# The end of a convolution mixer by token halves, with an activation that names the next function's table and an order edge on one product

## The chip, the cores and the metric

The kernel runs on one core of one Trainium2 chip. The metric is the device time of one execution in microseconds (us). The core has five engines with a queue each: TensorE (PE) multiplies matrices, VectorE (DVE), ScalarE (ACT) and GpSimd (POOL) work on vectors, and SyncE (SP) issues the transfers. Each takes its instructions in the order in which they stand in its queue, and waits on semaphores for what other engines hand it.

## The reference, cut to what matters

The network is a long chain of layers; the change touches the conformer mixer of its second block (and, by an order edge that moves nothing, one product of the first block's indexer). For 256 tokens and 1024 channels the mixer is

```python
a, g = jnp.split(h @ w_in + b_in, 2, axis=-1)
u = a * jax.nn.sigmoid(g)
u = lax.conv_general_dilated(u, w_dw[:, None, :], window_strides=(1,),
        padding=[(CONV_WIDTH - 1, 0)], feature_group_count=D_MODEL, ...) + b_dw
mu = jnp.mean(u32, axis=-1, keepdims=True)
var = jnp.mean(jnp.square(u32 - mu), axis=-1, keepdims=True)
u = (u32 - mu) * lax.rsqrt(var + LN_EPS) * ln_g + ln_b
return jax.nn.silu(u) @ w_out + b_out
```

So there is a product with 2048 outputs, a gate, a causal depthwise convolution of 31 taps per channel, a layer norm over the channels of each token, a Silu, and a second product.

## The kernel before, in words

The 1024 channels are eight blocks of 128, one channel per partition. All products are made in three passes, from a high and a low part of each operand (helper mm3, lines 203 to 205: high by high, high by low, low by high). Weights arrive through SyncE in pieces of 1 MB (tile raw, two buffers); ScalarE casts each half of a piece to its high part (L149) and VectorE subtracts that to get the low part (L152). For the last weights of the mixer (w2, w3) GpSimd does the subtraction.

The first product runs block by block. For each block TensorE sums a and g, ScalarE makes the sigmoid (tile sg, L1428) and VectorE the gated u (tiles ud, up, L1429). Blocks 0 to 3 are made in an earlier loop, in token halves, blocks 4 to 7 one after the other; the weights of block 7 have the tiles ws_12396 and ws_12399 in the listings below.

The 31 taps of the convolution are divided among the engines:

- VectorE has two lanes that it takes in turn, blocks 1 and 3, then blocks 2 and 4 and one tap of block 5: one instruction per tap over all 256 tokens (L1393, the first tap of a block L1395, the tap of block 5 L1397, tile part).
- GpSimd has block 0 and 14 taps of block 5 (tile pw).
- TensorE has blocks 6 and 7 and the last 16 taps of block 5, as products with diagonal matrices. ScalarE makes each diagonal matrix from the identity (tile diag, eight buffers, L1367 and L1377). Blocks 6 and 7 come out with channels on partitions (L1368: one product of 256 columns in two passes) and go to the tile cv by ScalarE (L1370). The 16 taps of block 5 come out with tokens on partitions: one product per token half, t0 and t1 (L1379).

At the end each block is turned to token rows by TensorE (stats, L1462 for one summand, L1465 for several); VectorE takes the statistics (bst, L1479 and L1481), ScalarE copies the rows out (tile rows, L1478 and L1482). norm_c makes mean and factor on VectorE and GpSimd and normalizes the rows on VectorE (L1552). silu_c turns them back on TensorE (L1558), ScalarE applies the Silu (L1562), and the second product follows (mm3 on ws of wcout).

What stands in which order is set by two things. A string PLAN lists the steps of the end: w is a weight to load, d some taps of VectorE, p and q the diagonal products of a block, t and r the row products of block 5, s the turning of a block. The framework then schedules each instruction by its own rules into the queue of its engine, as far as data, buffers and order edges allow: after(i, j) makes i follow j, and in_turn chains the products of the end on TensorE. Nothing else ties a diagonal matrix, a subtraction or a tap to its place in the text.

Of the kernel before, what the change touches and what calls it, by code (L numbers as in the profile page):

```python
# [9 lines left out]
F32 = mybir.dt.float32  # L10
# [4 lines left out]
AF = mybir.ActivationFunctionType  # L15
# [4 lines left out]
D = 1024  # L20
# [8 lines left out]
P_CW, P_CB, P_BA, P_BX, P_LAM, P_BIN, P_DB, P_LG, P_LB, P_DW = 0, 4, 5, 6, 7, 8, 10, 11, 12, 13  # L29
# [10 lines left out]


NTAP = (16, 16, 16, 16)
PLAN = "w0 w1 d64 p6: w2 d32 p7:20 s1 s2 s0 s6 q7:20 d999 t5:2 s7 r5:2 w3 s3 s4 s5"
ROWS = tuple(int(w[1]) for w in PLAN.split() if w[0] == "s")
LAG = 3
KACT = 1
GATE = 1
# [2 lines left out]
KS = 1  # L50
KQ = 14
WPOOL = 2
# [16 lines left out]
def _body(nc, tc, ctx, a, out, dbg):  # L69
# [17 lines left out]
    def ps(tag):  # L87
        return pp.tile([128, 512], F32, name=tag, tag=tag, bufs={"pm": 2, "pt": 2, "pa": 4}[tag])
# [69 lines left out]
    st = Stream()  # L158

    def after(i, j):  # L160
        tc.add_manual_dep(i.ins, j.ins.name, mybir.DependencyInfo(mybir.DependencyClass.NoSync, mybir.DependencyReason.DATA), reason="order")
# [36 lines left out]
    def cut(pair, c):  # L198
        return tuple(v.rearrange("p (c w) -> p c w", c=c) for v in pair)

    def mm3(o, wp, xp, first, last):
        (wh, wl), (xh, xl) = wp, xp
        nc.tensor.matmul(o, wh, xh, start=first, stop=False)  # L203
        nc.tensor.matmul(o, wh, xl, start=False, stop=False)  # L204
        nc.tensor.matmul(o, wl, xh, start=False, stop=last)  # L205

    def split_to(hi, lo, src):
        split_to.last = nc.scalar.activation(hi, src, AF.Copy)  # L208
# [112 lines left out]
    def rows_src(w, n):  # L321
        v = w.rearrange("(n c p) d -> n p c d", c=2, p=128)
        return [v[i] for i in range(n)]
# [5 lines left out]
    with ExitStack() as s1:  # L329
# [12 lines left out]
        def tmp(name, shape, bufs=2, dt=F32):  # L342
            return bp.tile(shape, dt, name=name, tag=name, bufs=bufs)
# [14 lines left out]
        ident = load_const("ident", [128, 128], a["ident"])  # L358
# [18 lines left out]
        pv = load_const("pv", [128, NPV, 8], a["pv"])  # L377
# [16 lines left out]
        r = rstd([xm[:NM]], D, bp, NM)  # L394
# [85 lines left out]
        az, sden, s2, acc_, mx, l8 = (ls[:, i, :] for i in range(6))  # L480
# [171 lines left out]
        scale = 96.0 ** -0.5  # L652
# [130 lines left out]
    with ExitStack() as s2:  # L783
# [259 lines left out]
        def first_queries():  # L1043

            p = [ps("pa") for _ in range(2)]
            pairs = [cut(pair, 4) for pair in st.units(a["wpq"][0])]
            for t in range(2):
                for ob in range(2):
                    o = p[ob][:, 256 * t:256 * t + 256]
                    s = slice(ob * 128, ob * 128 + 128)  # L1050
                    for c in range(8):
                        wh, wl = (v[:, c % 4, s] for v in pairs[c // 4])
                        v = xT[0].tiles[c // 4][:, c % 4, :, 128 * t:128 * t + 128]
                        if c == 7:
                            nc.tensor.matmul(o[:, 0:128], wl, v[:, 0], start=False, stop=False)
                        nc.tensor.matmul(o.rearrange("p (k t) -> p k t", k=2), wh, v, start=c == 0, stop=c == 7)
                        if c < 7:
                            nc.tensor.matmul(o[:, 0:128], wl, v[:, 0], start=False, stop=False)
                    dst = qT[:, ob, 128 * t:128 * t + 128]
                    nc.scalar.activation(dst, o[:, 128:256], AF.Copy)  # L1060
                    nc.vector.tensor_tensor(out=dst, in0=o[:, 0:128], in1=dst, op=ALU.add)
# [11 lines left out]
        for n in range(64):  # L1073
            cn = C[:, 2 * n:2 * n + 2, :]
            hb = cp.tile([128, 2, T], F32, name="hb", tag="hb", bufs=2)
            for u, pair in enumerate(st.units(a["peer_u"][n])):
                p = ps("pa")
                wh, wl = cut(pair, 8)
# [64 lines left out]
    with ExitStack() as s3:  # L1143
# [195 lines left out]
        cv = Q([128, 8, T], F32, "cv")  # L1339
# [13 lines left out]
        turn = {}  # L1353
# [6 lines left out]
        def dwconv_pe(b, k0, k1):  # L1360
            u = uslot(b)
            if k0 == 0:
                parts[b] = [cv[:, b, :]], ps("pm")
            p = parts[b][1]
            for k in range(k0, k1):
                dg = tmp("diag", [128, 128], 8)
                turn["act"] = nc.scalar.activation(dg, ident, AF.Copy, scale=pv[:, P_DW + k, b:b + 1])  # L1367
                in_turn(nc.tensor.matmul(p[:, :T], dg, u[:, k:k + T], start=k == 0, stop=k == 30))  # L1368
            if k1 == 31:
                nc.scalar.activation(cv[:, b, :], p[:, :T], AF.Identity, bias=pv[:, P_DB, b:b + 1])  # L1370
                parts[b] = parts[b][0]

        def dwconv_rows(b, k0, k1):
            u = uslot(b)
            for k in range(k0, k1):
                dg = tmp("diag", [128, 128], 8)
                turn["act"] = nc.scalar.activation(dg, ident, AF.Copy, scale=pv[:, P_DW + k, b:b + 1])  # L1377
                for t in range(2):
                    in_turn(nc.tensor.matmul(rows_at(b, t), u[:, k + t * 128:k + t * 128 + 128], dg, start=k == KQ + KS, stop=False))  # L1379

        def taps(lane):
# [49 lines left out]
        dsteps = together(VL)  # L1431
# [6 lines left out]
        order = []  # L1438
# [12 lines left out]
                return p[:, (i - 4) * 256 + t * 128:(i - 4) * 256 + t * 128 + 128]  # L1451
            return p[:, t * 128:t * 128 + 128]

        def stats(b):

            n = len(order)
            assert ROWS[n] == b
            order.append(b)
            for t in range(2):
                src = [v[:, t * 128:(t + 1) * 128] for v in parts[b]]  # L1460
                if len(src) == 1:
                    in_turn(nc.tensor.transpose(rows_at(b, t), src[0], ident))  # L1462
                    continue
                for i, v in enumerate(src):
                    in_turn(nc.tensor.matmul(rows_at(b, t), v, ident, start=i == 0 and b != 5, stop=i == len(src) - 1))  # L1465
            if n not in ENDS:
                return
            i = n
            f, n = ENDS[i]
            c = i // 2 - 1 if i < 6 else i - 4  # L1470
            for t in range(2):
                dst = rows[:, t, f * 128:(f + n) * 128]
                src = rows_at(b, t)
                if i == 3:
                    src = banks[0][t]
                elif i == 5:
                    src = banks[4][t].rearrange("p (b t c) -> p b t c", b=2, t=2)[:, :, t, :]
                    nc.scalar.activation(dst.rearrange("p (b c) -> p b c", b=2), src, AF.Copy)  # L1478
                    nc.vector.bn_stats(bst[:, t, c, :], dst)  # L1479
                    continue  # L1480
                nc.vector.bn_stats(bst[:, t, c, :], src)  # L1481
                nc.scalar.activation(dst, src, AF.Copy)  # L1482
# [29 lines left out]
        def run_steps(g, n=999):  # L1512
            for _ in range(n):
                if next(g, 0) == 0:
                    return
# [6 lines left out]
                taps_pool(5, 6, KQ)  # L1522
        wco = []

        srcs = rows_src(a["wcout"], 4)
        for w in PLAN.split():
            if w[0] == "w":
                st.gate = turn.get("act")
                wco.append(st.units(srcs[int(w[1:])], eng=nc.gpsimd, behind=turn["pool"]) if int(w[1:]) >= WPOOL else st.units(srcs[int(w[1:])]))
                st.gate = None  # L1530
            elif w[0] == "p":
                dwconv_pe(int(w[1]), 0, int(w[3:] or 31))
            elif w[0] == "q":
                dwconv_pe(int(w[1]), int(w[3:]), 31)
            elif w[0] == "r":
                dwconv_rows(int(w[1]), KQ + KS + int(w[3:] or 0), 31)
            elif w[0] == "t":
                dwconv_rows(int(w[1]), KQ + KS, KQ + KS + int(w[3:]))
            elif w[0] == "d":
                run_steps(dsteps, int(w[1:]))  # L1540
            else:
                stats(int(w[1:]))
        dump("cv", cv)
        def norm_c(t):
            mv = small.tile([128, 2], F32, name="mv", tag="mv", bufs=2)
            nc.vector.bn_aggr(mv, bst[:, t, :, :])
            rs = small.tile([128, 1], F32, name="rsc", tag="rsc", bufs=2)
            nc.vector.tensor_scalar(rs, mv[:, 1:2], 1e-5, None, ALU.add)
            nc.gpsimd.tensor_tensor(out=rs, in0=rs, in1=mhalf, op=ALU.pow)
            for half in range(2):  # L1550
                s = slice(half * 512, half * 512 + 512)
                nc.vector.tensor_scalar(rows[:, t, s], rows[:, t, s], mv[:, 0:1], rs, ALU.subtract, ALU.mult)  # L1552
# [10 lines left out]
                c = slice(4 * half, 4 * half + 4)  # L1563
                split_to(yT[0][:, c, t * 128:(t + 1) * 128], yT[1][:, c, t * 128:(t + 1) * 128], z)

        norm_c(0)
        silu_c(0)
        norm_c(1)
        acc, late = gemm_rows(yT, wco, 8, order=order, fill=(FILL, lambda: silu_c(1)))
# [236 lines left out]
```

## Time and profile before

| | us |
|---|---|
| median of 3 runs | 2092.8 |
| lowest and highest | 2091.31, 2092.88 |
| the profiled execution | 2094.42 |
| its span in the trace | 2092.6 |
| the mixer of the second block, in that span | about 1286 to 1393 |

The span is the time from the first to the last instruction in the trace; the profiled execution is 1.82 us longer than its span. TensorE is busy in 98% of the span, VectorE in 70%, ScalarE in 57%, GpSimd in 26%. Starts in the rows are us from the start of the span. "[2.13 <-DVE ud L1429]" at the end of a row says that the engine sat idle for 2.13 us before it, and that the last thing it waited for was VectorE's instruction of line 1429 on tile ud. Rows that run back to back are merged, with "xN" for their number.

### The profile page before, as it was taken

To read this page: it belongs to the slowest core of one execution; us is meant where nothing else is said; L and a number is where in the kernel's file an instruction comes from. 1 tells how busy PE (TensorE), PEld (TensorE's weight loads), DVE (VectorE), ACT (ScalarE), POOL (GpSimd) and SP (SyncE) were. 2 spreads that over 40 slices of the span, in tenths; PEclk is the share of its full clock that TensorE was granted. 3 is DMA by queue.
4 is the path that set the end of the run, shared out by engine and by line. 5 is a ranking of instruction groups with operands and counts; after the bars stand their busy time and mean duration, and the time that the engine had idled before them with its cause. 6 is when DMAs were issued, how large, how long until landed. Compare 5 with 4: busy or idle time off the path is not lost.

```text
span 2092.6 us, 29885 instructions
## 1 busy us (share of the span) xinstructions
PE 2045.3 (98%) x11342; PEld 1759.9 (84%) x11342; DVE 1462.1 (70%) x2624; ACT 1190.1 (57%) x1978; POOL 544.8 (26%) x431
## 2 busy tenths in 40 slices
PE   7999999999999999999999999989999999999998
PEld 7899988888898888888878888878887888887886
DVE  6675669999987766666666666966666665757564
ACT  5785445676776644444455555565555554655553
POOL 2000006787878344444300001920000000000000
PEclk9999999999999999999999999999999999999999
DMA  8783456666666766666667554226555554745551
GB/s 270 253 301 101 161 184 162 182 182 188 176 148 164 232 232 228 244 233 234 236 249 247 183 193 162 87 83 233 197 181 182 200 184 159 271 162 181 182 194 67
DMA packets 103440, 403.38 MB, mean 193 GB/s; under 512 B 31472, under 2 KB 33648, under 8 KB 71552
## 3 DMA queue, kind: packets, MB, share of 16 engines
q1 hardware_dynamic: 74880, 384.56, 53.8%
q0 software_dynamic: 28416, 16.91, 4.5%
q8 instruction: 89, 1.46, 0.3%
q14 instruction: 55, 0.45, 0.1%
HBM read 381.26 MB, written 18.96 MB: 191 GB/s over the span
## 4 chain that ended last, share of the span: by engine, by line
PE 81%; DVE 10%; ACT 4%; DMA 2%; issue 2%; POOL 1%; SPq 0%; DVEq 0%; POOLq 0%; ACTq 0%
PE pa L203 12%; PE pa L205 12%; PE pa L204 12%; PE pa L186 10%; PE pt L186 6%; PE pm L186 6%; PE pa L188 5%; DVE ws L152 3%; PE pt L188 3%; PE pm L188 3%; PE pm L203 2%; PE pm L205 2%; PE pm L204 2%; DVE pa L1393 2%; ACT ws L149 1%
## 5 line engine op out<-in xcount | busy, mean ns | idle before, releaser
L152 DVE TENSOR_TENSOR ws<-raw,ws 128x1024 fp32r<-128x1024 f32 (+1 forms) x661 | 819.1, 1245 | 430.9 <-ACT ws L149 424.7
L149 ACT ACTIVATE ws<-raw 128x1024 fp32r<-128x1024 f32 (+1 forms) x665 | 697.0, 1055 | 508.7 <-PE pa L205 263.3
L186 PE MATMUL pa<-xT,ws 128*128 128x512 f32 x1136 | 395.3, 396 | 0.4 <-ACT ws L149 0.4
L226 POOL TENSOR_TENSOR rr<-rs,mhalf 128x1 f32<-128x1 f32 (+1 forms) x36 | 31.5, 875 | 1191.6 <-DVE rs L224 1187.5
L188 PE MATMUL pa<-xT,ws 128*128 128x256 f32 x994 | 281.3, 283 | 1.7 <-DVE ws L152 1.7
L937 POOL DMA_INDIRECT gd<-gate,slot x128 | 227.6, 1778 | 88.4 <-DVE slot L932 36.2
L186 PEld LDWEIGHTS pa<-xT,ws 128*128 128x128 f32 x1136 | 205.8, 188 | 38.6 <-ACT ws L149 0.8
L204 PE MATMUL pa<-ws,ch 128*128 128x512 f32 x512 | 202.0, 395 | 0.0
L205 PE MATMUL pa<-ws,ch 128*128 128x512 f32 x512 | 201.8, 395 | 0.0
L203 PE MATMUL pa<-ws,ch 128*128 128x512 f32 x512 | 201.3, 395 | 0.0
L188 PEld LDWEIGHTS pa<-xT,ws 128*128 128x128 f32 x994 | 186.9, 188 | 9.2 <-DVE ws L152 4.6
L186 PE MATMUL pt<-xT,ws 128*128 128x512 f32 x512 | 190.7, 394 | 0.0
L186 PE MATMUL pm<-xT,ws 128*128 128x512 f32 x512 | 190.5, 394 | 0.0
L203 PE MATMUL pa<-ws,hT 128*128 128x512 f32 x352 | 139.3, 396 | 0.7 <-ACT hT L208 0.7
L205 PE MATMUL pa<-ws,hT 128*128 128x512 f32 x352 | 138.6, 394 | 0.3 <-DVE hT L209 0.3
L204 PE MATMUL pa<-ws,hT 128*128 128x512 f32 x352 | 138.4, 393 | 0.0
L188 PE MATMUL pm<-xT,ws 128*128 128x256 f32 x448 | 125.7, 281 | 0.0
L188 PE MATMUL pt<-xT,ws 128*128 128x256 f32 x448 | 125.7, 281 | 0.0
L205 PEld LDWEIGHTS pa<-ws,ch 128*128 128x128 f32 x512 | 96.4, 188 | 22.8 <-DVE ch L209 0.3
L203 PEld LDWEIGHTS pa<-ws,ch 128*128 128x128 f32 x512 | 96.4, 188 | 22.7
L204 PEld LDWEIGHTS pa<-ws,ch 128*128 128x128 f32 x512 | 96.4, 188 | 22.6 <-DVE ws L152 0.3
L186 PEld LDWEIGHTS pt<-xT,ws 128*128 128x128 f32 x512 | 96.0, 187 | 22.5 <-DVE hT L209 0.3
(481 smaller groups left out, 4223.4 us busy)
## 6 DMA issues: line engine op xcount, KB each, us to landing
raw<-in_ffn_dram SPq DMA_DIRECT2D x132, 1024.0 KB
raw<-in_peer_u_dram SPq DMA_DIRECT2D x64, 1024.0 KB
raw<-in_peer_v_dram SPq DMA_DIRECT2D x64, 1024.0 KB
raw<-in_win_dram SPq DMA_DIRECT2D x16, 1024.0 KB
x<-gd POOLq DMA_DIRECT2D x64, 256.0 KB
gain<-in_gains_dram SPq DMA_DIRECT2D x17, 512.0 KB
gd<-zero SPq DMA_DIRECT2D x16, 512.0 KB
gd<-zero SPq DMA_DIRECT2D x8, 1024.0 KB
```

Of the source, the lines that this page charges most:

```text
L149: i = nc.scalar.activation(hi, r, AF.Copy)
L152: self.last = (eng or nc.vector).tensor_tensor(out=lo, in0=r, in1=hi.bitcast(F32), op=ALU.subtract)
L186: nc.tensor.matmul(o, wp[0], v, start=first, stop=last)
L188: nc.tensor.matmul(o[:, 0:256], wp[1], v[:, 0:256], start=False, stop=False)
L203: nc.tensor.matmul(o, wh, xh, start=first, stop=False)
L204: nc.tensor.matmul(o, wh, xl, start=False, stop=False)
L205: nc.tensor.matmul(o, wl, xh, start=False, stop=last)
L226: nc.gpsimd.tensor_tensor(out=r2[:rows], in0=r[:rows], in1=mhalf[:rows], op=ALU.pow)
L937: i = nc.gpsimd.indirect_dma_start(gflat, bass.IndirectOffsetOnAxis(ap=slot[:, h, k:k + 1], axis=0), gate[:, h, k:k + 1], None, compute_op ...
L1393: nc.vector.scalar_tensor_tensor(out=o, in0=u, scalar=w, in1=acc, op0=ALU.mult, op1=ALU.add)
```

## The change

Three edits are in the diff.

1. The end by token halves. After block 7 is turned, the last 14 of block 5's 16 diagonal taps are made for t0 alone, then blocks 3, 4 and 5 are turned for t0; a new step u normalizes t0's rows and makes the 14 products of t1; then blocks 3, 4 and 5 are turned for t1. The 14 diagonal matrices now have to stay until t1 has used them: the first six lie in the diag buffers, the other eight in a tile named xn, which no other instruction holds at that time.
2. A Silu of one column (tile idle, L1573), which has a result that nobody reads, with an edge behind the last diagonal matrix (turn["act"]).
3. In the first block, the first_queries products of t0 get an edge behind the last product of mm3. The order on every engine there is the same as before.

norm_c and silu_c themselves only move up in the text. Later lines move too: L1367 becomes L1370, L1368 L1371, L1377 L1386, L1379 L1389, L1393 L1403, L1395 L1405, L1428 L1438, L1429 L1439, L1462 L1473, L1465 L1476, L1482 L1493, L1552 L1544, L1558 L1550, L1562 L1554.

```
-PLAN = "w0 w1 d64 p6: w2 d32 p7:20 s1 s2 s0 s6 q7:20 d999 t5:2 s7 r5:2 w3 s3 s4 s5"
+PLAN = "w0 w1 d64 p6: w2 d32 p7:20 s1 s2 s0 s6 q7:20 d999 t5:2 s7 r5:2 w3 s3:0 s4:0 s5:0 u5:2 s3:1 s4:1 s5:1"
...
-        def dwconv_rows(b, k0, k1):
+        kept = {}
+
+        def dwconv_rows(b, k0, k1, ts=(0, 1)):
             u = uslot(b)
             for k in range(k0, k1):
-                dg = tmp("diag", [128, 128], 8)
-                turn["act"] = nc.scalar.activation(dg, ident, AF.Copy, scale=pv[:, P_DW + k, b:b + 1])
-                for t in range(2):
+                if k not in kept:
+                    if len(kept) == 6:
+                        kept["xn"] = tmp("xn", [128, D], 1)
+                    n = len(kept) - 7
+                    kept[k] = kept["xn"][:, n * 128:n * 128 + 128] if n >= 0 else tmp("diag", [128, 128], 8)
+                    turn["act"] = nc.scalar.activation(kept[k], ident, AF.Copy, scale=pv[:, P_DW + k, b:b + 1])
+                dg = kept[k] if len(ts) == 1 else kept.pop(k)
+                for t in ts:
                     in_turn(nc.tensor.matmul(rows_at(b, t), u[:, k + t * 128:k + t * 128 + 128], dg, start=k == KQ + KS, stop=False))
...
-        def stats(b):
+        def stats(b, ts=(0, 1)):
...
-            for t in range(2):
+            for t in ts:
...
             elif w[0] == "r":
-                dwconv_rows(int(w[1]), KQ + KS + int(w[3:] or 0), 31)
+                dwconv_rows(int(w[1]), KQ + KS + int(w[3:] or 0), 31, (0,))
+            elif w[0] == "u":
+                norm_c(0)
+                idle = small.tile([128, 1], F32, name="idle", tag="idle", bufs=1)
+                after(nc.scalar.activation(idle, mhalf, AF.Silu), turn["act"])
+                dwconv_rows(int(w[1]), KQ + KS + int(w[3:] or 0), 31, (1,))
...
-                stats(int(w[1:]))
+                stats(int(w[1]), (int(w[3]),) if w[2:] else (0, 1))
...
-        norm_c(0)
         silu_c(0)
         norm_c(1)
...
+            behind = mm3.last
...
+                        i = nc.tensor.matmul(o.rearrange("p (k t) -> p k t", k=2), wh, v, start=c == 0, stop=c == 7)
+                        if t == 0:
+                            after(i, behind)
```

The scheduler puts more in another place than the text does. Three places matter.

VectorE, where the taps begin. Before, the two subtractions for block 7's weights (ws_12396, ws_12399) stand among the first taps (pa_12132 and pa_12134 are the two lanes' sums):

```order
L1395 TENSOR_SCALAR pa_12132<-ud_11797,pv_154 128x256
L152 TENSOR_TENSOR ws_12396<-raw_12394,ws_12396 128x1024
L1393 SCALAR_TENSOR_TENSOR pa_12132<-ud_11797,pv_154,pa_12132 128x256
L152 TENSOR_TENSOR ws_12399<-raw_12394,ws_12399 128x1024
L1429 SCALAR_TENSOR_TENSOR ud_11797<-pt_12096,pv_154,sg_12101 128x128
```

Now they stand behind the end of both first blocks' taps (cv) and the first taps of the next two blocks, in front of the four subtractions of w0 and w1 (ws_12455 to ws_12466):

```order
L1403 SCALAR_TENSOR_TENSOR cv_11795<-ud_11797,pv_154,pa_12132 128x256
L1403 SCALAR_TENSOR_TENSOR cv_11795<-ud_11797,pv_154,pa_12134 128x256
L1405 TENSOR_SCALAR pa_12132<-ud_11797,pv_154 128x256
L1405 TENSOR_SCALAR pa_12134<-ud_11797,pv_154 128x256
L152 TENSOR_TENSOR ws_12396<-raw_12394,ws_12396 128x1024
L152 TENSOR_TENSOR ws_12399<-raw_12394,ws_12399 128x1024
L152 TENSOR_TENSOR ws_12455<-raw_12453,ws_12455 128x1024
```

Between the two places stand 60 taps (L1393) and five gates (L1429). On TensorE block 7's product, which reads the low parts from its fifth product on, still stands in front of all diagonal products of blocks 6 and 7.

ScalarE, at the sigmoids of blocks 0 and 1 for the second half of the tokens (sg_12039 and sg_12042), among casts of weights. Before:

```order
L149 ACTIVATE ws_12234<-raw_12229 128x1024
L1428 ACTIVATE sg_12039<-pt_12034,pv_154 128x128
L149 ACTIVATE ws_12319<-raw_12317 128x1024
L149 ACTIVATE ws_12322<-raw_12317 128x1024
L1428 ACTIVATE sg_12042<-pt_12034,pv_154 128x128
L1404 ACTIVATE pw_11796<-ud_11797,pv_154 128x256
```

Now the idle Silu stands here, some 100 instructions ahead of the Silu of t0, with a table load on either side; the eight diagonal matrices of the tile xn have moved up to just before these rows (among the casts of ws_12154 to ws_12231), and with them the instruction that the idle Silu is tied to:

```order
L149 ACTIVATE ws_12234<-raw_12229 128x1024
L1438 ACTIVATE sg_12039<-pt_12034,pv_154 128x128
L149 ACTIVATE ws_12319<-raw_12317 128x1024
L1573 ACT_TABLE_LOAD
L1573 ACTIVATE idle_12820<-mhalf_69 128x1
L1438 ACT_TABLE_LOAD
L1438 ACTIVATE sg_12042<-pt_12034,pv_154 128x128
L1414 ACTIVATE pw_11796<-ud_11797,pv_154 128x256
```

The cast of ws_12322 has moved behind.

ScalarE, at the end of the mixer, in the changed kernel. The rows of t1 (from L1489 on the second time) stand ahead of the table load for the Silu of t0, which is still there:

```order
L1373 ACTIVATE cv_11795<-pm_12634,pv_154 128x256
L1386 ACTIVATE diag_12773<-ident_81,pv_154 128x128
L1489 ACTIVATE rows_11811<-pt_12755 128x256
L1493 ACTIVATE rows_11811<-pt_12804 128x128
L1493 ACTIVATE rows_11811<-pm_12747 128x128
L1489 ACTIVATE rows_11811<-pt_12755 128x256
L1493 ACTIVATE rows_11811<-pt_12804 128x128
L1493 ACTIVATE rows_11811<-pm_12748 128x128
L1554 ACT_TABLE_LOAD
```

The copies of rows from pa (L1493), which before stood behind block 7's cv, and the casts of w3, which stood behind the last diagonal matrix, have moved up: the copies to between the diagonal matrices of block 5, the casts to between the first ones of block 7. On TensorE t0's turning (L1550) stands behind all products of t1. The queues of GpSimd and SyncE read as before.

## Rows read from the trace of the kernel before

**Rows 1.** The page: busy time of engines, and the chain by engine.

```profile
PE 2045.3 (98%) x11342; PEld 1759.9 (84%) x11342; DVE 1462.1 (70%) x2624; ACT 1190.1 (57%) x1978; POOL 544.8 (26%) x431
...
PE 81%; DVE 10%; ACT 4%; DMA 2%; issue 2%; POOL 1%; SPq 0%; DVEq 0%; POOLq 0%; ACTq 0%
```

**Rows 2.** Chain of waits, 1300 to 1395: start, us, what ended last.

```profile
1340.68 7.54 DVE ws L152 x4
1348.22 22.73 DVE pa L1393 x58
...
1371.73 1.01 DVE part L1397
```

**Rows 3.** Timeline of TensorE, from block 7's product to the second product.

```profile
1329.16 0.28 PE L203 MATMUL pm<-xT,ws 128*128 128x256 f32 x1
...
1334.80 0.28 PE L205 MATMUL pm<-xT,ws 128*128 128x256 f32 x1
1335.70 22.29 PE L1368 MATMUL pm<-up,diag 128*128 128x256 f32 x102 [0.62 <-ACT sg L1428]
...
1364.13 0.38 PE L1379 MATMUL pm<-diag,up 128*128 128x128 f32 x2
...
1365.85 6.42 PE L1379 MATMUL pm<-diag,up 128*128 128x128 f32 x56
...
1373.66 0.39 PE L1465 MATMUL pm<-ident,part 128*128 128x128 f32 x2
1377.14 1.94 PE L1558 MATMUL pt<-ident,rows 128*128 128x128 f32 x8 [3.10 <-DVE rows L1552]
...
1380.69 0.80 PE L203 MATMUL pa<-ws,xT 128*128 128x512 f32 x1
```

**Rows 4.** Timeline of VectorE, the places of block 7's subtractions and of the others.

```profile
1309.34 1.47 DVE L152 TENSOR_TENSOR ws<-raw,ws 128x1024 fp32r<-128x1024 f32 x1
1310.74 0.47 DVE L1393 SCALAR_TENSOR_TENSOR pa<-ud,pv,pa 128x256 f32<-128x256 f32 x1
1311.13 1.92 DVE L152 TENSOR_TENSOR ws<-raw,ws 128x1024 fp32r<-128x1024 f32 x1
...
1319.32 0.48 DVE L1429 SCALAR_TENSOR_TENSOR ud<-pt,pv,sg 128x256 f32<-128x256 f32 x1 [0.85 <-ACT sg L1428]
...
1339.31 0.98 DVE L1395 TENSOR_SCALAR pa<-ud,pv 128x256 f32<-128x256 f32 x2
```

**Rows 5.** Timeline of TensorE behind a wait, in the product of block 4.

```profile
1314.16 0.39 PE L203 MATMUL pt<-xT,ws 128*128 128x256 f32 x1 [2.13 <-DVE ud L1429]
...
1315.02 0.41 PE L205 MATMUL pt<-xT,ws 128*128 128x256 f32 x1
1315.23 0.41 PE L203 MATMUL pt<-xT,ws 128*128 128x256 f32 x1
...
1318.14 0.28 PE L205 MATMUL pt<-xT,ws 128*128 128x256 f32 x1
```

**Rows 6.** Windows: length, busy us by engine, granted clock, DMA share, GB/s.

```profile
1315.00:1320.00 5.00, 5.00 (x33) 5.00 (x32) 4.15 (x11) 2.25 (x3) 4.76 (x4) 0.70 0.48 197
```

**Rows 7.** Timeline of ScalarE: table loads, and what follows them.

```profile
1286.42 1.28 ACT L1428 ACT_TABLE_LOAD   x1
1287.71 0.37 ACT L1428 ACTIVATE sg<-pt,pv 128x128 f32<-128x128 f32 x1
...
1304.68 1.06 ACT L149 ACTIVATE ws<-raw 128x1024 fp32r<-128x1024 f32 x1 [0.37 <-PE pm L205]
...
1375.76 1.28 ACT L1562 ACT_TABLE_LOAD   x1
1378.27 1.85 ACT L1562 ACTIVATE y<-pt,pv 128x128 f32<-128x128 f32 x5 [1.22 <-PE pt L1558]
```

**Rows 8.** Tile raw, 1340 to 1347: w3's issue (ns min/median/max, first to last start).

```profile
L133 SPq DMA_DIRECT2D raw<-in_wcout_dram x1: 368/368/368, 1343.8 to 1343.8; - x1
```

**Rows 9.** Transfers, 1340 to 1360: rate in 40 slices of 0.5 us.

```profile
GB/s 0 0 0 0 0 0 0 0 0 82 147 205 426 418 434 344 57 0 229 33 213 426 377 442 344 33 0 0 0 0 0 0 0 0 0 33 0 0 0 0
```

More of the change, by code (lines that the diff above doesn't have):

```diff
@@ L42 @@
 NTAP = (16, 16, 16, 16)
-PLAN = "w0 w1 d64 p6: w2 d32 p7:20 s1 s2 s0 s6 q7:20 d999 t5:2 s7 r5:2 w3 s3 s4 s5"
-ROWS = tuple(int(w[1]) for w in PLAN.split() if w[0] == "s")
+PLAN = "w0 w1 d64 p6: w2 d32 p7:20 s1 s2 s0 s6 q7:20 d999 t5:2 s7 r5:2 w3 s3:0 s4:0 s5:0 u5:2 s3:1 s4:1 s5:1"
+ROWS = tuple(int(w[1]) for w in PLAN.split() if w[0] == "s" and w[2:] != ":1")
 LAG = 3
@@ L204, in mm3 @@
         nc.tensor.matmul(o, wh, xl, start=False, stop=False)
-        nc.tensor.matmul(o, wl, xh, start=False, stop=last)
+        mm3.last = nc.tensor.matmul(o, wl, xh, start=False, stop=last)
     def split_to(hi, lo, src):
@@ L1055, in first_queries @@
                             nc.tensor.matmul(o[:, 0:128], wl, v[:, 0], start=False, stop=False)
-                        nc.tensor.matmul(o.rearrange("p (k t) -> p k t", k=2), wh, v, start=c == 0, stop=c == 7)
+                        i = nc.tensor.matmul(o.rearrange("p (k t) -> p k t", k=2), wh, v, start=c == 0, stop=c == 7)
+                        if t == 0:
+                            after(i, behind)
                         if c < 7:
@@ L1452, in rows_at @@
             return p[:, t * 128:t * 128 + 128]
-        def stats(b):
-            n = len(order)
-            assert ROWS[n] == b
-            order.append(b)
-            for t in range(2):
+        def stats(b, ts=(0, 1)):
+            n = ROWS.index(b)
+            if b not in order:
+                assert n == len(order)
+                order.append(b)
+            for t in ts:
                 src = [v[:, t * 128:(t + 1) * 128] for v in parts[b]]
@@ L1470, in stats @@
             c = i // 2 - 1 if i < 6 else i - 4
-            for t in range(2):
+            for t in ts:
                 dst = rows[:, t, f * 128:(f + n) * 128]
@@ L1523, in _body @@
         wco = []
[L1525 to L1535, printed above, removed]
-                dwconv_rows(int(w[1]), KQ + KS + int(w[3:] or 0), 31)
[L1537 to L1541, printed above, removed]
-                stats(int(w[1:]))
-        dump("cv", cv)
         def norm_c(t):
@@ L1564, in silu_c @@
                 split_to(yT[0][:, c, t * 128:(t + 1) * 128], yT[1][:, c, t * 128:(t + 1) * 128], z)
-        norm_c(0)
+        srcs = rows_src(a["wcout"], 4)
+        for w in PLAN.split():
+            if w[0] == "w":
+                st.gate = turn.get("act")
+                wco.append(st.units(srcs[int(w[1:])], eng=nc.gpsimd, behind=turn["pool"]) if int(w[1:]) >= WPOOL else st.units(srcs[int(w[1:])]))
+                st.gate = None
+            elif w[0] == "p":
+                dwconv_pe(int(w[1]), 0, int(w[3:] or 31))
+            elif w[0] == "q":
+                dwconv_pe(int(w[1]), int(w[3:]), 31)
+            elif w[0] == "r":
+                dwconv_rows(int(w[1]), KQ + KS + int(w[3:] or 0), 31, (0,))
[4 more added lines that the diff above has]
+                dwconv_rows(int(w[1]), KQ + KS + int(w[3:] or 0), 31, (1,))
+            elif w[0] == "t":
+                dwconv_rows(int(w[1]), KQ + KS, KQ + KS + int(w[3:]))
+            elif w[0] == "d":
+                run_steps(dsteps, int(w[1:]))
+            else:
+                stats(int(w[1]), (int(w[3]),) if w[2:] else (0, 1))
+        dump("cv", cv)
         silu_c(0)
```

## The prediction, made before the changed kernel was run

> **What bounds the kernel now.** I read the page first, for the engine that sets the pace: TensorE is busy in 98% of the span and 81% of the chain that ended last [rows 1]. What makes TensorE late, or leaves it idle, makes the kernel late; for other engines the question is only whether TensorE waits for them. Then the chain of waits over the mixer's end, 1300 to 1395 us: here VectorE ends last, with four subtractions (7.54 us, 1.885 each), 58 taps (22.73 us), part until 1372.74 and the normalizing [rows 2]. A reader could conclude that TensorE has time to spare here. The timeline of TensorE says otherwise: block 7's product runs from 1329.16 to 1335.08, the 51 diagonal products of blocks 7 and 6 follow 0.62 us later, then block 5's rows and the turnings, until 1374.05, without a pause that matters [rows 3]. The last turning ends 1.3 us behind VectorE's part. The two are level; whichever comes later sets the end. The true pause is 3.10 us before the turning back of t0's rows, for normalized rows, and the second product starts at 1380.69 [rows 3].
>
> **The change part by part.** Edit 3 changes no engine's order: nothing. Edit 1 is meant to take the pause of 3.10 us, edit 2 to put a table load into idle time. But before, the load at 1375.76 ended at 1377.04, and the Silu then waited another 1.22 us for TensorE [rows 7]: there was nothing to gain from it alone. And the order shows that it still stands in front of the Silu of t0, with two more loads elsewhere. So I follow what the scheduler moved.
>
> *Step 1, VectorE: when are block 7's low parts there?* Before, their two subtractions began at 1309.34 and 1311.13 and cost 1.40 (to the next start) and about 1.85 (1.92 less the same overlap) [rows 4]. They now stand behind the first tap of the second pair of blocks, which ended at 1339.31 + 0.98 = 1340.29 [rows 4]. VectorE reaches that point 3.25 us earlier, since the two are gone from ahead of it. Against that, ScalarE has two loads of 1.28 us and a one-column activation (estimate 0.2; the smallest one of the rows, 128 columns, takes 0.35 to 0.37) in front of a sigmoid that VectorE's gate needs: 2.8 us. One cast of 1.06 us has moved from ahead of that sigmoid to behind it [rows 7], and VectorE's wait of 0.85 us at 1319.32 [rows 4], for a product which was held up before it, has room to go. I take 2.8 - 1.06 - 0.85 = 0.9 us of delay; the ends are 0 and 2.8. The low parts start at 1340.29 - 3.25 + 0.9 = 1337.9 and are there at 1339.8 and 1341.7, at the 1.885 us that the four behind them took [rows 2]. The eight diagonal matrices among the casts (0.3 us each, estimate from 128 columns at 0.37) go into ScalarE's waits for TensorE there, as the 0.37 ahead of a cast shows one [rows 7]; they are inside the same ends.
>
> The Trainium skill, ScalarE: Activation LUTs, section "What ACT_TABLE_LOAD costs", gives 1283 ns for the load and about 1380 ns of drain on top, 2.66 us per switch. In this trace the load that starts at 1286.42 is followed by its sigmoid at 1287.71, 1.29 us on [rows 7]: no drain on top. By that section the two loads would cost 2.8 us more; by the row, nothing more. The row decides.
>
> *Step 2, TensorE: block 7's product.* Its fifth product reads the low part. TensorE gets there by 1329.16 + 4 x 0.12 = 1329.6 or earlier, and now waits until 1339.8, 10 us or more. Queued behind it on TensorE, in order, is everything to the end of the mixer. Then 44 products are left. Their pitch before was (1334.80 - 1329.16) / 47 = 0.12 us [rows 3], 5.3 us in all. But after a wait of only 2.13 us at 1314.16, the pitch was 0.21 (1315.02 to 1315.23) and the granted clock had a mean of 0.70 in 1315 to 1320, the lower of the two levels, 1.2 GHz, for part of it; the next row at full pitch is 1318.14 [rows 5, 6]. So after 10 us of idling I charge 3.5 us at half speed, which loses 1.75 us (ends: 0, if the clock doesn't fall, and 2, the 4.0 us from 1314.16 to 1318.14). The second low part comes in time: 20 products and more lie between. The product ends at 1339.8 + 5.3 + 1.75 + 0.2 = 1347.1 instead of 1335.1: **12.0 us late**.
>
> *Step 3, the diagonal products.* Same instructions, 22.29 us for 51 products, 0.437 each [rows 3], and ScalarE makes a matrix in less: all shifts by 12.0. One new danger: w3's casts now stand after the third and the tenth matrix that ScalarE makes here. w3's transfer was issued at 1343.8 [rows 8], behind w0's subtractions, and its bytes flowed from about 1344.5 to 1348.5 [rows 9], 4.7 us from issue to end. w0's subtractions now end at 1341.7 + 2 x 1.885 = 1345.5, so w3 is there at 1350.2, its cast done at 1351.3. TensorE has the eight matrices of the eight buffers, made ahead, plus three: 11 x 0.437 = 4.8 us from 1347.7, until 1352.5. Hidden by 1.2 us; without that cover up to 2 us. I take 0. Block 5's first row product moves from 1364.13 to 1376.1.
>
> *Step 4, the end by halves.* From 1364.13 to 1374.05 TensorE did 9.9 us of row products and turnings [rows 3]. The same work, in another order, ends at 1386.0. ScalarE now copies two rows from pa between matrices that TensorE needs; they wait for VectorE's statistics behind part, which ends at 1372.74 + 0.9 = 1373.6 [rows 2], 2.5 us before TensorE arrives at 1376.1: 0 (end: 1). t0's turning back stands behind t1's products and turnings. By then t0's rows are normalized: 14 products of t1 (14 x 6.42 / 28 = 3.2 us) and their turnings lie between, and before, from the last turning to the normalized rows, both halves together took 1377.14 - 1374.05 = 3.1 us [rows 3]. TensorE goes on at once: the 3.10 us are gone, and 1377.14 becomes 1386.0, 8.9 late. But the Silu also has t1's three copies and the table load ahead of it: before, copies and statistics took from 1374.05 to 1375.76, 1.7 us, for both halves [rows 3, 7]; I take 1.4 (ends 1.0 and 1.7), and 1.28 for the load. Silu at 1386.0 + 1.4 + 1.28 = 1388.7, before 1378.27: **10.4 late**. The second product follows it as before.
>
> *Sum.* Behind it TensorE is busy without a pause, at 98% to the end of the program, so the delay stays: +10.4 us. The profiled execution's 2094.42 becomes 2104.8; it lies 1.6 above the median of 2092.8, which becomes **2103.2 us**. Ends of the unknown terms: step 1 from -0.9 to +1.9, step 2 from -1.75 to +0.25, step 3 to +2, step 4 from -0.4 to +1.3.
>
> **The rivals.**
>
> - *TensorE is late, but less.* The clock keeps its full level, or VectorE loses nothing to the loads: 10.4 - 1.75 - 0.9 = 7.7, 2100.5 us; with later stages taking up another 2 us, 2098.5. For it: the stretch of low clock differs from wait to wait. Against: the wait is five times the one that lowered it [rows 5].
> - *TensorE is starved again.* w3 comes late among the diagonal matrices, by 1 to 2 us, or the subtractions beside GpSimd take longer than their mean: 2104.5 to 2107. The cover of 1.2 us is thin.
> - *A table load delays its activation beyond its own time.* ScalarE's sigmoid and VectorE's gate then come later, with all behind them; at the upper end of step 1 (2.8 instead of 0.9) this gives 2105.1 us. The sigmoid that follows its load by 1.29 us speaks against it [rows 7]. By the Trainium skill's price (ScalarE: Activation LUTs, "What ACT_TABLE_LOAD costs") it would be 2106.
> - *Not slower.* Block 7's low parts are not what TensorE waits for, or the wait is under about 2 us: then VectorE's chain still ends the taps at 1372.74 plus the delay of 0.9 [rows 2], TensorE ends at 1374.05 plus as much, and t0's turning back follows without the 3.10 us: Silu at 1374.05 + 0.9 + 1.4 + 1.28 = 1377.6, 0.6 early: 2092.2 us, between 2091 and 2095. For it: the chain names VectorE, not TensorE, in this stretch. Against: the product does read the low parts, and they stand behind 60 taps of 0.39 us, some 24 us of work. It decides from a wait in block 7's product of under 2 us.
>
> **How the numbers follow.** The forecast (2101.5 to 2105) gets 0.60, the smaller delay 0.15, the starved case 0.09, the longer table load 0.04, not slower 0.12. Of this last one, a third is faster by over 0.2% (4.2 us, about what a measurement of this kernel can tell from no change): 0.03; the rest, 0.09, is within 0.2%. Slower: 0.88. The range leaves out a tenth on each side: 2098.5 to 2107.
>
> **What would show it.** In the profile of the changed kernel: on TensorE, a wait of 10 us or more for VectorE's subtraction (L152) in block 7's product, ending near 1340, then a pitch of 0.21; the diagonal products (now L1371) starting near 1347.7; t0's turning back (L1550) near 1386 and ended by ScalarE or TensorE, not by the normalizing; ScalarE with two loads at about 1305 to 1308 and a third in front of the Silu. Wrong would be a wait in block 7's product of under 2 us, a start of the diagonal products before 1340, or the delay shrinking behind 1390.

## The result, and the profile after

The changed kernel takes 2105.1 us (median of 4 runs, 2101.92 to 2107.85), the kernel before 2092.84 in the same comparison: ratio 1.0058, 95% interval 1.0046 to 1.0070, so 9.6 to 14.7 us more. Run once more beside the experiments it gave 1.0060 (1.0045 to 1.0076). Forecast were 2103.2 us, within 2098.5 to 2107.

The profiled execution is the fastest of the four. Its span is 2100.1 us, 7.5 more than before. It is 3.0 us ahead of the earlier profile when the mixer starts: the mixer's first turning begins at 1283.47 instead of 1286.45, and 2.7 of these 3.0 us arise in the first 130 us, in which nothing is changed. To compare, I measure from that turning (L1500, now L1511) to VectorE's first instruction behind the second product: 1392.89 - 1286.45 = 106.44 us before, 1400.28 - 1283.47 = 116.81 now. Before, and the end now:

```profile
1286.45 0.66 PE L1500 MATMUL pt<-ident,y 128*128 128x128 f32 x4 [0.70 <-ACT y L1497]
1392.89 1.39 DVE L1575 TENSOR_TENSOR xn<-pa,gain 128x512 f32<-128x512 f32 x2 [1.99 <-PE pa L205]
...
1400.28 1.37 DVE L1590 TENSOR_TENSOR xn<-pa,gain 128x512 f32<-128x512 f32 x2 [1.91 <-PE pa L205]
```

**The mixer takes 10.4 us more**, and later products keep the shift: 10.4 less the 3.0 are the 7.5 by which the spans differ, to a tenth.

TensorE in the changed kernel, around block 7's product (start, us, engine, line, operation; idle time ahead of it and its releaser):

```profile
1283.47 0.66 PE L1511 MATMUL pt<-ident,y 128*128 128x128 f32 x4 [0.68 <-ACT y L1508]
...
1336.17 0.80 PE L205 MATMUL pm<-xT,ws 128*128 128x256 f32 x2 [13.35 <-DVE ws L152]
1336.77 0.41 PE L203 MATMUL pm<-xT,ws 128*128 128x256 f32 x1
1336.98 0.41 PE L204 MATMUL pm<-xT,ws 128*128 128x256 f32 x1
1337.19 0.41 PE L205 MATMUL pm<-xT,ws 128*128 128x256 f32 x1
...
1339.82 0.28 PE L203 MATMUL pm<-xT,ws 128*128 128x256 f32 x1
1339.94 0.27 PE L204 MATMUL pm<-xT,ws 128*128 128x256 f32 x1
...
1343.81 6.53 PE L1371 MATMUL pm<-up,diag 128*128 128x256 f32 x28 [0.62 <-ACT sg L1438]
```

The same product ran through in [rows 3]. It now stops at its fifth product for 13.35 us, and what ends the wait is VectorE's subtraction. Then the pitch is 0.21 us until 1339.5, and 0.12 again. The diagonal products start 60.3 us behind the first turning, where it was 49.3.

VectorE, at the sigmoid and at the subtractions:

```profile
1304.58 0.35 DVE L1439 SCALAR_TENSOR_TENSOR ud<-pt,pv,sg 128x128 f32<-128x128 f32 x1 [1.78 <-ACT sg L1438]
...
1333.13 0.99 DVE L1405 TENSOR_SCALAR pa<-ud,pv 128x256 f32<-128x256 f32 x2
1334.02 12.59 DVE L152 TENSOR_TENSOR ws<-raw,ws 128x1024 fp32r<-128x1024 f32 x6
```

Six subtractions where [rows 2] has four, and block 7's are the first two. What holds VectorE up earlier is ScalarE, with the idle Silu between two table loads:

```profile
1301.37 1.28 ACT L1573 ACT_TABLE_LOAD   x1
1302.66 0.20 ACT L1573 ACTIVATE idle<-mhalf 128x1 f32<-128x1 f32 x1
1302.88 1.28 ACT L1438 ACT_TABLE_LOAD   x1
1304.17 0.37 ACT L1438 ACTIVATE sg<-pt,pv 128x128 f32<-128x128 f32 x1
...
1347.38 1.06 ACT L149 ACTIVATE ws<-raw 128x1024 fp32r<-128x1024 f32 x1 [1.56 <-DMA raw<-in_wcout_dram]
...
1371.41 1.20 ACT L1493 ACTIVATE rows<-pa 128x512 f32<-128x512 f32 x2 [0.46 <-DVE bst L1492]
...
1383.73 0.28 ACT L1493 ACTIVATE rows<-pm 128x128 f32<-128x128 f32 x1 [0.39 <-DVE bst L1492]
1384.03 1.28 ACT L1554 ACT_TABLE_LOAD   x1
1385.33 1.86 ACT L1554 ACTIVATE y<-pt,pv 128x128 f32<-128x128 f32 x5
```

The last three rows are the mixer's end: a third load, and this one does delay the Silu, which starts when it ends (in [rows 7] it waited for TensorE). The copies of rows at 1371.41 stand ahead of four matrices and of block 7's cv. TensorE at the same place:

```profile
1374.18 0.94 PE L1389 MATMUL pm<-diag,up 128*128 128x128 f32 x6 [1.29 <-ACT cv L1373]
...
1382.98 0.39 PE L1476 MATMUL pm<-ident,part 128*128 128x128 f32 x2
1383.20 1.04 PE L1550 MATMUL pt<-ident,rows 128*128 128x128 f32 x8
1386.89 0.66 PE L1550 MATMUL pt<-ident,rows 128*128 128x128 f32 x4 [2.65 <-ACT y L1554]
1387.75 0.79 PE L203 MATMUL pa<-ws,xT 128*128 128x512 f32 x1 [0.21 <-ACT xT L208]
```

The 3.10 us ahead of t0's turning back in [rows 3] are gone, as the change means it to be. The windows give the granted clock (columns as in [rows 6]):

```profile
1325.00:1330.00 5.00, 0.00 (x0) 0.00 (x0) 5.00 (x14) 0.00 (x0) 4.76 (x4) 0.60 0.00 0
1330.00:1335.00 5.00, 0.00 (x0) 0.00 (x0) 5.00 (x12) 0.00 (x0) 4.76 (x4) 0.50 0.00 0
1335.00:1340.00 5.00, 3.83 (x19) 3.83 (x20) 5.00 (x3) 0.00 (x0) 4.84 (x4) 0.54 0.15 12
1340.00:1345.00 5.00, 4.38 (x33) 4.03 (x33) 5.00 (x4) 0.90 (x3) 4.84 (x3) 1.00 0.79 306
```

TensorE does nothing for two windows, the clock goes to its lower level (0.50, 1.2 GHz), and stays there for 3.4 us of work.

### The profile page after: what moved, and what is told of

Read it like the earlier page. It is cut to its first block, busy times and chain, and to the rows that moved or that the text cites. A ratio compares the mean times of both kernels' runs of the same rounds, so it can differ in the third digit from the quotient of the medians.

```text
span 2100.1 us, 29876 instructions
## 1 busy us (share of the span) xinstructions
PE 2042.2 (97%) x11342; PEld 1757.0 (84%) x11342; DVE 1461.3 (70%) x2624; ACT 1188.0 (57%) x1981; POOL 539.0 (26%) x431
## 4 chain that ended last, share of the span: by engine, by line
PE 84%; DVE 7%; ACT 3%; issue 2%; DMA 2%; POOL 1%; SPq 0%; DVEq 0%; POOLq 0%; ACTq 0%
PE pa L203 13%; PE pa L205 12%; PE pa L204 12%; PE pa L186 11%; PE pt L186 6%; PE pm L186 6%; PE pa L188 5%; PE pm L188 3%; PE pt L188 3%; PE pm L203 2%; PE pm L205 2%; PE pm L204 2%; DVE ws L152 2%; DVE pa L1403 2%; PE pm L959 1%
```

## The experiments

All ratios are to the kernel before, run beside them. "Mixer" is the time defined above, from the profiled execution: 106.44 before, 116.81 changed. Of each edit the lines that matter are shown, and the remarks behind # are added here.

**1. Without the idle Silu.**

```
-                idle = small.tile([128, 1], F32, name="idle", tag="idle", bufs=1)
-                after(nc.scalar.activation(idle, mhalf, AF.Silu), turn["act"])
```

> The change without the idle Silu alone (edits 1 and 3 stay). The scheduler then leaves block 7's two subtractions among VectorE's first taps. Theory (the low parts come late, since the idle Silu moved ScalarE's and VectorE's order): no wait over 2 us in block 7's product; the diagonal products start near 1335; the Silu of t0 at about 1374.1 + 0.3 + 1.4 + 1.3 = 1377, 1 us before the kernel before; time 2090.5 to 2093.5, ratio to before 0.999 to 1.0005. Rival (the halves themselves cost, by 14 kept matrices and by copies of rows between matrices): the wait in block 7's product is gone, but the time stays 4 us or more above before, ratio 1.002 or more.

Measured: 1.0003 (0.9994 to 1.0011), and in a second comparison 0.9992 (0.9983 to 1.0001); expected again was:

> The change without the idle Silu once more, beside the kernel that has it in its right place: 1 to 3 us slower than that one, ratio to before 0.9995 to 1.0005.

There is no wait in block 7's product, and the diagonal products start 47.6 us behind the first turning. The halves and the kept matrices cost nothing that can be measured: the rival falls, and with it every account in which edit 1 alone is to blame. (The copies of rows are not tested by this: without the idle Silu the scheduler leaves them behind the matrices.) My expectation for the second comparison fell: beside the kernel of experiment 7 this one was not slower (0.9992 against 0.9998). One activation of one column makes the difference, by where it pushed the others. The end then looks as forecast: the Silu starts 88.34 us behind the first turning, 1.96 behind the last one, of which 1.28 are the load.

**2. The changed kernel with block 7's subtractions early.** Both loads stay, and TensorE's order is the same. On ScalarE the scheduler moves w3's casts and the copies of rows back as well, so that their share goes with that of the subtractions; experiment 5 tells them apart.

```
+        after(tapped[14], st.last)      # tapped: VectorE's taps, in order; st.last: block 7's second subtraction
```

> The changed kernel with all its edits and both extra table loads, and one order edge more: the 15th tap of VectorE stands behind block 7's second subtraction. TensorE's order is that of the changed kernel. Theory (late low parts): no wait over 2 us in block 7's product; VectorE still loses 1 to 2 us at the sigmoid behind the two loads, and has no slack at the end: ratio to before 0.9995 to 1.001, 2092 to 2095. Rival (the two table loads on ScalarE and what they delay are the cost): ratio 1.004 or more, 2101 or above, as in the changed kernel.

Measured: 1.0017 (1.0008 to 1.0025). The wait in block 7's product is gone, and with it about seven tenths of the loss: late low parts are the main cost. The remainder, 0.8 to 2.5 thousandths, is more than I expected, and for another reason. VectorE wasn't later: its last tap ended 83.97 us behind the first turning, before the change 85.27. TensorE got there first (the mixer is 108.82 us here, 2.4 above before):

```profile
1368.53 0.87 PE L1474 MATMUL pt<-ident,cv 128*128 128x128 f32 x2 [3.49 <-DVE cv L1403]
...
1370.47 2.77 PE L1389 MATMUL pm<-diag,up 128*128 128x128 f32 x12
1373.03 2.71 PE L1389 MATMUL pm<-xn,up 128*128 128x128 f32 x16
```

t0's turnings wait for VectorE's last tap, and t1's 14 products stand behind them: work that TensorE did while VectorE was still at its taps [rows 3] now comes after, and after an idle 3.49 us at half speed (1370.47 to 1375.74, 5.3 us for 14 products; at the pitch of [rows 3] they take 3.2; the granted clock is 0.54 from 1370 to 1375). These 2.1 us are a cost of the halves, and they show only where TensorE is ahead and its clock falls. In experiment 7 it waits 2.42 us at the same place, and the 14 products keep their pitch:

```profile
1374.36 0.72 PE L1473 MATMUL pt<-ident,cv 128*128 128x128 f32 x2 [2.42 <-DVE cv L1403]
...
1375.59 1.50 PE L1389 MATMUL pm<-diag,up 128*128 128x128 f32 x12
1376.93 1.95 PE L1389 MATMUL pm<-xn,up 128*128 128x128 f32 x16
```

**3. The kept matrices behind block 7's sigmoid.** One tie more on ScalarE, which brings the idle Silu and the subtractions to where the change wants them, with 31 table loads as before.

```
+                    after(turn["act"], turn["sg"])      # turn["sg"]: the last sigmoid
```

> The changed kernel with the matrices of block 5 that t1 uses again tied behind block 7's sigmoid. The idle Silu then follows them, with one table load for both Silus (31 loads, as before), and VectorE's order is that of before up to the taps' end. Theory (late low parts, else the change does as it is meant): the first diagonal product near 1336, TensorE waits up to 1 us more for matrices; the Silu of t0 follows the copies of rows without a load: 1376 or so, 2 us ahead of before; ratio 0.998 to 1.0, 2089 to 2093. Rival (halves cost by themselves): ratio 1.002 or more.

Measured: 1.0009 (1.0001 to 1.0018); mixer 102.53 in its profile. No wait in block 7's product, so the main theory stands. My forecast of a gain fell: the profiled execution has one (the Silu 0.55 us behind the last turning), the median doesn't. TensorE there waits 0.40 us for a matrix and 1.20 for VectorE's last tap. Why the other runs are slower is open.

**4. The idle Silu alone, on the kernel before.**

```
+                idle = small.tile([128, 1], F32, name="idle", tag="idle", bufs=1)
+                after(nc.scalar.activation(idle, mhalf, AF.Silu), turn["act"])
```

> The kernel before with the idle Silu alone, behind the last diagonal matrix; there it stays at the mixer's end, ahead of w3's casts and the copies of rows. Theory (the load was hidden: it ended 1.22 us before the Silu could start): nothing, ratio 0.9995 to 1.0005, and the Silu of t0 still waits for TensorE. Rival (the table load counts): 1.3 us less, ratio 0.9994 or below, or a loss where the load stands in front of the copies of rows.

Measured: 1.0012 (1.0003 to 1.0021), mixer 107.15. No gain: the load was hidden, as [rows 7] had it. The small loss just clears the interval, and the profile has it too: it is the rival's second branch, the load and w3's casts stand ahead of the copies of rows, and TensorE's pause for normalized rows grew from 3.10 to 3.77 us.

**5. The kernel before with block 7's subtractions late.** The suspected cost alone, without any edit of the change.

```
+            st.hold = tapped[59] if b == 7 else None     # in units: after(each subtraction, st.hold)
```

> The kernel before, with no edit of the change, but with block 7's two subtractions tied behind the end of the first lanes' taps on VectorE (60th tap). Theory (late low parts are the cost): TensorE waits 9 to 11 us in block 7's product, until about 1339; the mixer takes 8 to 11 us more than before, ratio 1.004 to 1.0055. Rival (the cost needs the halves, the copies of rows or the table loads as well): the wait is there, but the mixer's end moves by less than 4 us, ratio under 1.002.

Measured: 1.0049 (1.0034 to 1.0065); mixer 117.08.

```profile
1339.30 0.80 PE L208 MATMUL pm<-xT,ws 128*128 128x256 f32 x2 [10.46 <-DVE ws L153]
...
1388.66 1.06 PE L1564 MATMUL pt<-ident,rows 128*128 128x128 f32 x8 [2.08 <-DVE rows L1558]
```

No edit of the change is in it; TensorE's and GpSimd's orders, and the number of table loads, are as before. Besides the subtractions the scheduler moves little, above all a gate, a sigmoid and two copies of rows. These copies stand between matrices here too, and cost little: TensorE waits 0.45 us for block 7's cv, 0.34 before. The wait for the low part is 10.46 us, and the mixer is as long as in the changed kernel. (The sum is not the same: the half speed behind the wait lasts 5.8 us here and 3.4 there, and 2.08 us ahead of t0's turning back remain.) Low parts that come late are enough for the whole cost, and with experiment 2 this settles the cause.

**6. The wait filled.** 105 spare products keep TensorE busy ahead of block 7's; their results are overwritten.

```
+                for k in range(spare if u == 0 else 0):
+                    nc.tensor.matmul(p[0][:, :n], wh[:, k % 4, 0:128], rhs[0][:, k % 4, off:off + n], start=True, stop=True)
```

> The changed kernel with 105 products more ahead of block 7's product, into the same accumulator, which the real product then starts anew: they fill some 12.5 us of TensorE's wait, and do nothing else. Theory (of the delay, 1.75 us are the lower clock behind the wait): the pitch is 0.12 us from the first product behind the low part on, and the diagonal products start 1.5 to 2 us earlier than in the changed kernel, against the start of the mixer; time 1 to 2.5 us less than the changed kernel's. Rival (the clock costs nothing on balance): the same start, no change.

Measured: 1.0061 (1.0046 to 1.0077), as the changed kernel beside it:

> The changed kernel itself, beside the others: ratio to before 1.0045 to 1.007, a wait of 12 to 14 us in block 7's product.

That one measured 1.0060 (1.0045 to 1.0076), with a wait of 13.36 us and a mixer of 116.88. So the forecast of 1 to 2.5 us less fell: the two times can't be told apart. The profile shows the gain and where it went:

```profile
1327.24 12.62 PE L270 MATMUL pm<-xT,ws 128*128 128x256 f32 x105
...
1341.35 0.51 PE L205 MATMUL pm<-xT,ws 128*128 128x256 f32 x2 [1.02 <-DVE ws L152]
...
1347.46 5.02 PE L1373 MATMUL pm<-up,diag 128*128 128x256 f32 x22 [0.62 <-ACT sg L1440]
1355.17 19.23 PE L1373 MATMUL pm<-up,diag 128*128 128x256 f32 x80 [2.69 <-ACT diag L1372]
```

```profile
1353.77 1.06 ACT L149 ACTIVATE ws<-raw 128x1024 fp32r<-128x1024 f32 x1 [4.31 <-DVE pa L1405]
```

The diagonal products start 58.92 us behind the first turning instead of 60.34: the lower clock had cost 1.4 us. But then TensorE uses up its eleven matrices, and waits 2.69 us while ScalarE, held at w3's cast, makes none. (The tap that the row names can't release a cast; the cast needs w3's transfer, which was issued at 1347.4.) In the changed kernel the cast ended 64.97 us behind the first turning, here 66.29, 1.3 later, and TensorE came 1.4 earlier: that is the 2.7. w3's transfer took 6.3 us from its issue, in the changed kernel 5.1; why is open. The half speed had covered this wait: taking one away brought out the other.

**7. The idle Silu behind t0's copies of rows.** The version that the experiments point to; no load is left in front of the Silu of t0.

```
-                after(nc.scalar.activation(idle, mhalf, AF.Silu), turn["act"])
+                after(nc.scalar.activation(idle, mhalf, AF.Silu), turn["rows"])     # turn["rows"]: the last copy of rows
```

> The changed kernel with one tie moved: the idle Silu stands behind t0's last copy of rows, not behind the last matrix. The order then has it at the mixer's end, its table load between t0's and t1's copies, and no load in front of the Silu of t0; block 7's subtractions are early again. Theory: VectorE and TensorE as before the change until 1373; the Silu of t0 starts 0.7 to 1.2 us behind the last turning, 1 to 1.3 us earlier than without the idle Silu; ratio to before 0.998 to 1.0. Rival (the load holds t1's copies up, or the Silu waits for something else): no gain over the kernel without the idle Silu.

Measured: 0.9988 (0.9979 to 0.9997). Run again:

> The kernel with the idle Silu behind t0's copies, once more, for its gain over before: ratio 0.998 to 0.9997. If the first result was chance, the interval holds 1.

0.9998 (0.9989 to 1.0007). The place of the load is right in both profiles:

```profile
1376.92 0.28 ACT L1493 ACTIVATE rows<-pm 128x128 f32<-128x128 f32 x1
1377.22 1.28 ACT L1573 ACT_TABLE_LOAD   x1
1378.51 0.20 ACT L1573 ACTIVATE idle<-mhalf 128x1 f32<-128x1 f32 x1
1379.03 0.38 ACT L1489 ACTIVATE rows<-pt 128x256 f32<-128x256 f32 x1 [0.31 <-PE pt L1473]
...
1380.31 1.85 ACT L1554 ACTIVATE y<-pt,pv 128x128 f32<-128x128 f32 x5
```

The Silu follows the last turning by 0.55 us, against 1.96 without the idle Silu; the mixer is 104.44 in this profile, 2.0 us below the kernel before. (In the repetition it is 100.48, and 103.54 without the idle Silu, both with a faster stretch on VectorE that the last section explains: 3 us apart.) 2 us are a tenth of a percent, and by the expectation above the first result may be chance: the second interval holds 1. In that second comparison the kernel without the idle Silu had 0.9992, so the medians don't show the 3 us either. It is a clear gain over the change, and none over the kernel before, or over leaving the idle Silu out, that I would claim.

**8. The turnings alone in halves.** All 28 products, t1's 14 among them, stay ahead of t0's turnings; the idle Silu is tied as in experiment 7.

```
-                dwconv_rows(int(w[1]), KQ + KS + int(w[3:] or 0), 31, (0,))
+                dwconv_rows(int(w[1]), KQ + KS + int(w[3:] or 0), 31)
...
-                dwconv_rows(int(w[1]), KQ + KS + int(w[3:] or 0), 31, (1,))
```

> The end by halves with the turnings alone: all 28 products of block 5 stay ahead of t0's turnings, as before the change, no matrix is kept for t1; idle Silu behind t0's copies of rows. It tells what t1's 14 products in the pause give. Theory (they fill the pause, so TensorE isn't idle there and its clock stays up): here TensorE pauses 2 to 3 us in front of t0's turning back, the second product starts at the lower clock in the runs in which the pause lowers it, and the time lies 1 to 3 us above that of the kernel with the products in the pause; ratio to before 0.999 to 1.0005. Rival (only the earlier start of t0's chain counts): as fast as that kernel or up to 1 us faster, ratio 0.9975 to 0.999.

Measured: 1.0003 (0.9994 to 1.0012), mixer 106.78. TensorE pauses 1.57 us among t1's turnings and 1.08 us ahead of t0's turning back. The products of t1 in the pause are worth about 2 us in the profiles (106.78 against 104.44). The medians of the same comparison don't tell the two apart (1.0003 and 0.9998, each within 0.0009), so they don't rule out the rival.

## Why the prediction was right, point by point

*What bounds.* Right, and shown by experiment 5: VectorE's name in the chain hid that TensorE was level with it, and a wait of 10.46 us on TensorE, with next to nothing else changed, made the mixer 10.6 us longer.

*Step 1.* The place was right, the delay too large. Behind the first turning, the low parts were forecast to start at 1337.9 - 1286.45 = 51.45 us and started at 1334.02 - 1283.47 = 50.55: the 0.9 us that I charged for the loads came out as nothing. VectorE did wait 1.78 us for the sigmoid, but its later wait of 0.85 us [rows 4] shrank to 0.21, and the subtractions around it were cheaper. The six subtractions then took 12.59 / 6 = 2.1 us each, not 1.885.

*Step 2.* The wait was forecast at 10 us or more and is 13.35: TensorE arrived 3.8 us earlier, since its own wait of 2.13 us [rows 5] had gone, and the half speed behind it. (VectorE's gate came 1.3 us earlier there, and eight products of block 5 now stand ahead of the one that had waited; neither the section on the change nor the prediction has this.) That cost nothing, as the other side sets the end of a wait. The lower clock was charged with 1.75 us and cost 1.4 by experiment 6. The diagonal products started 60.34 us behind the first turning, 0.9 earlier than forecast (1347.7 - 1286.45 = 61.25).

*Step 3.* No starvation, as forecast, but the margin was not the 1.2 us that I gave: eleven matrices last TensorE until 60.34 + 4.8 = 65.1, and w3's cast ended at 64.97. The twelfth matrix is made only behind that cast, and TensorE lost 0.2 us there. So the cover was gone; experiment 6 shows what lies behind it.

*Step 4.* The 3.10 us went, and the table load is on the path, both as forecast. Of the terms, that of ScalarE's copies between the matrices was taken as 0 and is 0.95: TensorE waits 1.29 us for block 7's cv, before 0.34. The 2.5 us of slack that I gave them were counted to the end of VectorE's statistics, without the copies (1.2 us) and the four matrices that ScalarE still makes ahead of cv. The last turning ended at 99.89, 0.3 later than forecast (1386.0 - 1286.45 = 99.55). Copies and load took 1.96 us from there, where I had 2.7, and the Silu came at 101.85, 0.4 early (102.25).

*Sum.* 10.4 us forecast, 10.0 found at the Silu (101.85 against 91.81) and 10.4 at the end of the second product. The errors of the terms, up to 0.95, cancel: that the sum is better than they are is luck. And the sum is that of the mixer. The medians differ by 12.3 us (9.6 to 14.7 by the interval), so some 1.9 us are not located: both traces of the changed kernel are of the fastest execution of their four.

*The rivals.* Of "late, but less" one half came true, as the loads cost VectorE nothing, and the other didn't, as the clock fell. "Starved again" didn't come in the changed kernel, but came in experiment 6; its range, 2104.5 to 2107, has no sum behind it (w3 late by 1 to 2 us gives 2104.2 to 2105.2). "Not slower" held that VectorE would cover the wait; experiments 1 and 5 rule it out. The longer table load falls: the sigmoid started 1.29 us after its load (1302.88 to 1304.17). By the price that the Trainium skill gives for a switch (ScalarE: Activation LUTs, "What ACT_TABLE_LOAD costs") it would have been 2.66, and this trace doesn't agree.

## What to carry to other kernels

An edge that says "not before this" says nothing on "not long after": where a scheduler fills queues by its own reckoning, read the new order of every engine, and look for an instruction that another engine waits for (here a subtraction of 2 us) behind a block of work that nobody waits for. Filler belongs behind something that is itself late, as experiment 7 ties it. And a split by halves moves work behind the waits of the first half: where the engine with that work is ahead of the one it waits for, look at what follows the wait (experiment 2 lost 2.1 us there to the lower clock, experiment 7 nothing).

## What the runs showed of the hardware

VectorE's four subtractions of w0 and w1 (two SBUF inputs each) take 7.54 us before [rows 2], 7.90 in experiment 7, and 4.62 in its repetition, which is the same kernel. (They take 4.62 in both traces of experiment 1 too, and 7.20 and 6.65 in experiments 2 and 3.) VectorE in experiment 7 and in its repetition:

```profile
1343.30 7.90 DVE L152 TENSOR_TENSOR ws<-raw,ws 128x1024 fp32r<-128x1024 f32 x4
...
1339.18 4.62 DVE L152 TENSOR_TENSOR ws<-raw,ws 128x1024 fp32r<-128x1024 f32 x4
```

GpSimd in the repetition, beside its usual 2.62 us for two of these additions:

```profile
1333.30 2.62 POOL L1422 TENSOR_TENSOR pw<-pw 128x512 f32<-128x512 f32 x2
...
1337.98 6.96 POOL L1422 TENSOR_TENSOR pw<-pw 128x512 f32<-128x512 f32 x2
```

So one of the two engines runs and the other stands. Which one hangs on little: behind the first turning, GpSimd's two additions start at 52.01 us in both executions, VectorE's subtractions at 53.89 in experiment 7 and at 53.21 in the repetition, and VectorE's last tap ends at 85.29 and 81.33. In the repetition VectorE is there first: GpSimd's second addition starts at 53.36 and ends at 58.96, behind all four subtractions. In experiment 7 that addition is first and takes its usual 1.27 us, and VectorE's first subtraction takes 1.83 instead of 1.21. The Trainium skill, SBUF — State Buffer, section "Who interferes with whom", says that a VectorE instruction with two SBUF inputs contends with a GpSimd instruction that reads SBUF, and that the order of issue decides which of them blocks; the trace agrees.

And the clock: after a wait of about 2 us for the same gate, the products came at half speed in the kernel before [rows 5], but at full speed in experiment 1's execution, where the diagonal products start 1.6 us earlier (47.64 against 49.25 us behind the first turning). The length of the wait doesn't tell which: at this place 2.02 us lowered the clock in experiment 7, and 2.12 us left it up in experiment 3. So the mixers of single profiles compare only where both pieces are alike. In the kernel before and in experiments 4, 7 and 8 the clock fell and the subtractions took 7.5 to 7.9 us; in experiment 1, its repetition and the repetition of experiment 7 neither was so. Runs of one kernel scatter: of the 11 runs of experiment 7, the six with a mean granted clock of 0.998 took 2088.05 to 2089.85 us, the five with 0.996 or 0.997 2090.75 to 2095.69. What made up each of these times is not shown, as only one of the eleven has a trace.
